# Output projection by seven products over four row pairs, and seven products of a weight pair gathered in one PSUM bank

## The chip, the cores and the metric

The kernel runs on one core of one Trainium2 chip. The metric is device time in microseconds (us) of one execution; smaller is better. Durations inside the execution come from one execution recorded by the hardware profiler.

## The reference, cut to what matters

A decoder block for one sequence of 1024 positions and D = 1024 channels, all in float32:

```python
h = rms_norm(x, norm_g)
proj = h @ w_in                      # u, g_rnn, q, k, v, g_attn, m_rnn, m_attn
u = causal_depthwise_conv(u, conv_w, conv_b)
y_rnn  = rg_lru(u, ...) * silu(g_rnn)
y_attn = sliding_window_attention_with_sinks(q, k, v, sinks) * silu(g_attn)
merged = sigmoid(m_rnn) * (y_rnn @ w_rnn_out) + sigmoid(m_attn) * (y_attn @ w_attn_out)
x = x + merged @ w_o
return rms_norm(x, final_norm_g)
```

## The kernel before, in words

**Precision.** Every float32 operand of a matrix product is split into a high part `h` (rounded to float32r by a ScalarE copy, L427) and a low part `l` (VectorE, `src - h`, L428). One 128x128 by 128x512 block product is then three matmuls: h·h, h·l, l·h.

**Pairs.** The weights of the input projection and of the two branch projections are cut into pairs. A pair is a 2x2 arrangement of blocks A11, A12, A21, A22 (128 output channels by 512 inputs each), and the right side is a 2x2 arrangement B11 ... B22 (512 inputs by 512 positions, each 4 tiles). `Pair.run` (L522) computes the 2x2 result by seven block products instead of eight, after Winograd: left sums S1 to S4 (L477), right sums T1 to T4 (L1004), seven products (L500, 12 matmuls each), and additions of products. Before the change these additions are five VectorE adds (u2, u3, c22, c21, c12) and one ScalarE copy (L517, of the first product), and a pair uses five PSUM banks, a to e. There are 32 such pairs: 8 `ug`, 2 `mr`, k, v, 4 `q`, 4 `ga`, 4 `ma`, 4 `zr` and 4 `za`. The right sides of one matrix (7 names x 4 tiles x 2 parts = 56 buffers) are built once and used by all its pairs: one for h, one for y_rnn (`zr`), one for y_attn (`za`).

**Merge.** `z_tail` (L1028) multiplies each finished block of `zr` and `za` with a gate loaded from DRAM (L1032) and, for `za`, adds it onto the `zr` block (L1041). That gives 16 tiles `MG[k, hf]`: channel tile k, half hf of the positions.

**Output projection.** The last stage (L1141 to L1174) splits all of MG (`mh`, `ml`) and of w_o (`Wh`, `Wl`), then goes through eight row blocks r of 128 positions. For each half c of the output channels it makes 8 block products of three matmuls into one bank (L1166, `three` at L567), adds x onto them (L1168), and after both halves it computes the root mean square (squares at L555 or L557, sum L561, root L563, reciprocal L564), scales (L1171) and stores (L1173). That is 8 x 2 x 8 x 3 = 384 matmuls.

**Order.** Nothing is issued in program order. Every operation is handed to a planner (`Plan.run`, L145) which lists it with its cost, its inputs and a priority, and writes out a fixed order for each engine; `TUNE` holds priorities and buffer limits, and `orders` the sequence of pairs and attention units. For work on TensorE the planner adds 1000 ns of slack after any input from another engine (L313). Buffers are 100 tiles of 128x512 in SBUF and 8 PSUM banks. Weight blocks are loaded through POOL's queue, everything else through SP's.

Of the kernel before, what the change touches and what calls it, by code (L numbers as in the profile page):

```python
# [11 lines left out]
F32R = mybir.dt.float32r  # L12
# [5 lines left out]
S = 1024  # L18
D = 1024
P = 128  # L20
# [12 lines left out]
    'm': (29, 2, 3),  # L33
# [4 lines left out]
    'zg': 3,  # L38
    'raw': 4,
    'raws': 9,  # L40
    'S': 4,
    'wc': 10,
    'B': 12,
    'psw': 67,
    'psk': 0,
    'Y': 8,
    'ld': 9,
    'lds': 21,
    'kv': 8,
    'kvs': 4,  # L50
    'qt': 4,
    'qts': 1,
    'P': 17,
    'AO': 22,
    'AOs': 12,
    'xo': 24,
    'lru0': 136,
    'xos': 11,
    'prep': 256,
    'att': 73,  # L60
    'val': 13,
    'gate': 1500,
    'lru': -1570,
    'qk': -147,
    'comb': 346,
    'ztl': -331,
    'xof': 47,
    'gzr': 21,
    'gza': 21,
    'gwo': 11,  # L70
    'gxo': 3,
    'gt': -6,
    'seven': 'ra',
    'mgd': 0,
# [268 lines left out]
def hybrid_block_kernel(ctx: ExitStack, tc: tile.TileContext, x, wall, wo, bd, vec, gfin,  # L343
# [16 lines left out]
                "P": (16, 0, 0, TUNE["P"]), "AO": (32, 0, 0, TUNE["AOs"]), "Y": (64, 0, 0, TUNE["Y"]), "zy": (TUNE["zy"], 0, 0, 0), "zg": (TUNE["zg"], 0, 0, 0), "wo": (32, 0, 0, TUNE["Y"]), "ld": (TUNE["ld"], 0, 0, TUNE["lds"]),  # L360
# [3 lines left out]
    def buf(cls, shape=None, dt=F32, name=None):  # L364
        return Buf(sp, "s2", cls, shape or [P, HF], dt, name or cls)
# [68 lines left out]
    def tt(dst, a, b, op, prio=0, eng=None):  # L434
        (eng or EW)(lambda e: e.tensor_tensor(dst.t, a.t, b.t, op=op), HF, [a, b], [dst], prio)  # L435
# [25 lines left out]
    class Pair:  # L461
# [3 lines left out]
        def __init__(self, i, comb, prio=None, cls="raw", by="POOL"):  # L465
            self.i, self.comb, self.prio, self.cls, self.A = i, comb, TUNE["prep"] if prio is None else prio, cls, {}
            self.W = {}
            self.by = by

        def raw(self, name):  # L470
            if name not in self.A:
                t = self.A[name] = buf(self.cls, name=name)
                b = ("A11", "A21", "A22", "A12").index(name)
                DMA(lambda: t.t, lambda: wall[self.i, b], 1 << 18, [], [t], self.prio, by=self.by)
            return self.A[name]

        def left(self, name):  # L477
            raw, prio, A = self.raw, self.prio, self.A
            if name[0] != "S":
                return raw(name)  # L480
            if name == "S1":
                return A["S1"]
            src = A[name] = buf("S", name=name)
            if name == "S2":
                s1 = A["S1"] = buf("S", name="S1")
                tt(s1, raw("A21"), raw("A22"), ADD, prio)
                tt(src, s1, raw("A11"), SUB, prio)
# [26 lines left out]
        def p1(self):  # L514
            self.a, self.c1 = bank("pair"), slot("p1")
            self.product(0, self.a, "A11", "B11", True)
            ACT(lambda q: q.copy(self.c1.t, self.a.t), HF, [self.a], [self.c1])  # L517

        def p2(self):
            self.product(2, self.a, "A12", "B21", False)  # L520
# [192 lines left out]
    def lru(c, C):  # L713
        (u0, u1), g = C
# [6 lines left out]
        hs = [None, None]  # L721
        for h, u in ((0, u0), (1, u1)):
# [24 lines left out]
            r, i, t, tg = (slot(n) for n in ("r", "i", "t", "tg"))  # L747
# [14 lines left out]
            gg = g[h]  # L762
            ACT(lambda e, tg=tg, gg=gg: e.activation(tg.t, gg.t, AF.Silu), HF, [gg], [tg], tset=SILU)
# [377 lines left out]
    WO = whole_from(lambda k, h: [((lambda: wo[k * P : (k + 1) * P, HALF[h]]), [])], [ahead(len(ids), TUNE["gwo"])], TUNE["comb"], "wo")  # L1141
    for h in range(2):
        for k in range(KT):
            WO(k, h)
    AO = {}
    for hf in range(2):
        for k in range(KT):
            AO[k, hf] = buf("AO", dt=F32R, name="mh")
            m = MG[k, hf]
            MG[k, hf] = buf("AO", dt=F32R, name="ml")  # L1150
            split_buf(AO[k, hf], MG[k, hf], m)
    gf_b = [load("xo", "gf_b") for _ in range(2)]
    for q in range(2):
        DMA(lambda q=q: gf_b[q].t, lambda q=q: gfin[HALF[q]].partition_broadcast(P), 1 << 18, [ahead(len(ids), TUNE["gxo"])], [gf_b[q]])
    for r in range(NB):
        xh = [load("xo", "xo") for _ in range(2)]
        for c in range(2):
            DMA(lambda c=c, xh=xh, r=r: xh[c].t, lambda c=c, r=r: x[r * P : (r + 1) * P, HALF[c]], 1 << 18,
                [ahead(len(ids), TUNE["gxo"])], [xh[c]], TUNE["xof"])
        w = slice(r % 4 * P, r % 4 * P + P)  # L1160
        for c in range(2):
            ps = bank("o")
            for k in range(KT):
                h, l = AO[k, r // 4], MG[k, r // 4]
                bh, bl = WO(k, c)
                PE(lambda ps=ps, h=h, l=l, w=w, bh=bh, bl=bl, k=k: three(ps, h, l, w, bh, bl, k == 0, k == KT - 1), 3,  # L1166
                   [h, l, bh, bl], [ps])
            tt(xh[c], ps, xh[c], ADD, 0, DVE)  # L1168
        rs = rstd_of(xh)
        for c in range(2):  # L1170
            DVE(lambda v, c=c, xh=xh, rs=rs: v.scalar_tensor_tensor(xh[c].t, xh[c].t, rs.t, gf_b[c].t, op0=MUL, op1=MUL), HF,  # L1171
                [xh[c], rs, gf_b[c]], [xh[c]], ptr=1)
            DMA(lambda c=c, xh=xh, r=r: out[r * P : (r + 1) * P, HALF[c]], lambda c=c, xh=xh: xh[c].t, 1 << 18, [xh[c]],  # L1173
                [("out", (r, c))])  # L1174
# [62 lines left out]
```

## Time and profile before

| | |
|---|---|
| Time, median of 3 runs | 901.39 us (901.3 to 901.75) |
| Time of the profiled execution | 901.53 us |
| Its span, first to last instruction | 899.8 us |
| PE busy | 874.7 us (97%) |
| VectorE (DVE) busy | 774.4 us (86%) |
| ScalarE (ACT) busy | 599.9 us (67%) |
| Mean granted TensorE clock | 0.99 |

The span is 1.7 us shorter than the time of the same execution; sums below are made in the span and then shifted. PE counts as busy while any matmul is in flight, and a matmul lasts longer than the distance to the next, so the rate is read from start to start.

### The profile page before, as it was taken

The page shows a single profiled execution, that of the slowest core. Times are in us where ns is not written, and L with a number is a line of the kernel's source. Part 1 is how long each engine was busy: PE and PEld are TensorE (multiplying, and loading weights), DVE is VectorE, ACT ScalarE, POOL GpSimd, SP SyncE. Part 2 cuts the span into 40 slices and gives each one's busy share as a digit, 9 for nine tenths or more (in the row PEclk, how much of TensorE's full clock was granted, in tenths as well). Part 3 has the DMA queues.
Part 4 walks back from the last instruction along what each step waited for, and adds up shares of the span by engine and source line. Part 5 has one row for each costly group of instructions (what it writes and reads, how often), then busy time and mean ns, then how long its engine had stood idle before and what let it go on. Part 6 is the DMA issues. An engine that isn't in the chain of part 4 may idle for free.

```text
span 899.8 us, 13035 instructions
## 1 busy us (share of the span) xinstructions
PE 874.7 (97%) x4088; PEld 721.8 (80%) x4088; DVE 774.4 (86%) x1579; ACT 599.9 (67%) x1232; POOL 72.9 (8%) x131
## 2 busy tenths in 40 slices
PE   4999999999999999999999999999999989999996
PEld 3778888878887888888888888888888868888885
DVE  6996999999996998888888888789999999897643
ACT  7655996996847777896498999999751444334000
POOL 2101010101000010011000000001100200000000
PEclk9999999999999999999999999999999979999999
DMA  9202146345641665256666445553857621682311
GB/s 327 104 34 83 58 119 173 111 140 145 164 129 48 194 193 139 72 138 213 171 173 188 132 130 176 146 158 89 268 184 244 207 74 50 208 297 78 117 47 47
DMA packets 86884, 129.75 MB, mean 144 GB/s; under 512 B 10656, under 2 KB 40224, under 8 KB 86816
## 3 DMA queue, kind: packets, MB, share of 16 engines
q1 hardware_dynamic: 77216, 97.47, 35.0%
q0 software_dynamic: 9600, 31.46, 12.1%
q8 instruction: 32, 0.52, 0.2%
q14 instruction: 36, 0.29, 0.1%
HBM read 87.21 MB, written 41.68 MB: 143 GB/s over the span
## 4 chain that ended last, share of the span: by engine, by line
PE 63%; DVE 3%; ACT 3%; issue 1%; DVEq 0%
PE pair L508 15%; PE pair L509 15%; PE pair L510 15%; PE o L569 3%; PE o L570 3%; PE o L568 3%; PE ps_s L899 3%; PE ptp L933 3%; PE po L947 1%; PE po L946 1%; ACT sm L914 1%; ACT sm L922 1%; DVE wl L428 1%; DVE cu L728 0%; ACT ph L427 0%
## 5 line engine op out<-in xcount | busy, mean ns | idle before, releaser
L418 POOL DMA_DIRECT2D A<-in_wall_dram x120 | 64.5, 538 | 676.6 <-PE pair L510 169.4
L427 ACT CAST wh<-S 128x512 fp32r<-128x512 f32 x128 | 78.3, 616 | 41.2 <-DVE S L435 27.6
L428 DVE TENSOR_TENSOR wl<-S,wh 128x512 fp32r<-128x512 f32 x128 | 87.6, 686 | 7.9 <-ACT wh L427 6.7
L435 DVE TENSOR_TENSOR c<-pair,u 128x512 f32<-128x512 f32 x96 | 65.6, 686 | 7.0 <-PE pair L510 6.4
L428 DVE TENSOR_TENSOR wl<-A,wh 128x512 fp32r<-128x512 f32 x96 | 65.9, 687 | 1.7 <-ACT wh L427 1.1
L427 ACT CAST wh<-A 128x512 fp32r<-128x512 f32 x96 | 59.3, 617 | 12.1 <-PE pair L510 6.3
L914 ACT ACTIVATE sm<-sm,nm 128x256 f32<-128x256 f32 (+1 forms) x128 | 61.9, 487 | 1.8 <-DVE nm L907 1.6
L922 ACT ACTIVATE sm<-sm,dn 128x256 f32<-128x256 f32 (+1 forms) x128 | 53.9, 489 | 1.8 <-DVE dn L919 0.9
L907 DVE CUSTOM_DVE_ANT_0 sm<-ps_s,mask_t,sink_t 128x256 f32<-128x256 f32 (+1 forms) x128 | 53.8, 459 | 1.0 <-PE ps_s L899 1.0
L509 PE MATMUL pair<-B21l,wh 128*128 128x512 f32 x128 | 51.2, 400 | 1.1 <-DVE B21l L428 1.1
L508 PE MATMUL pair<-B11h,wh 128*128 128x512 f32 x128 | 51.7, 404 | 0.5 <-DVE B12l L424 0.5
L508 PE MATMUL pair<-B21h,wh 128*128 128x512 f32 x128 | 51.9, 406 | 0.3 <-ACT B21h L427 0.3
L509 PE MATMUL pair<-T2l,wh 128*128 128x512 f32 x128 | 50.0, 391 | 1.9 <-DVE T2l L428 1.9
L563 ACT ACTIVATE sd<-ss,eps_t 128x1 f32<-128x1 f32 x16 | 4.3, 289 | 71.1 <-DVE ss L561 71.1
L508 PE MATMUL pair<-B22h,wh 128*128 128x512 f32 x128 | 51.0, 398 | 0.8 <-DVE c L435 0.8
L510 PE MATMUL pair<-B21h,wl 128*128 128x512 f32 x128 | 50.9, 398 | 0.0
L508 PE MATMUL pair<-T3h,wh 128*128 128x512 f32 x128 | 50.7, 396 | 0.0
L508 PE MATMUL pair<-T4h,wh 128*128 128x512 f32 x128 | 50.7, 396 | 0.0
L508 PE MATMUL pair<-T1h,wh 128*128 128x512 f32 x128 | 50.6, 396 | 0.0
L509 PE MATMUL pair<-B11l,wh 128*128 128x512 f32 x128 | 50.5, 394 | 0.0
L510 PE MATMUL pair<-B11h,wl 128*128 128x512 f32 x128 | 50.3, 393 | 0.0
L508 PE MATMUL pair<-T2h,wh 128*128 128x512 f32 x128 | 50.1, 392 | 0.0
(222 smaller groups left out, 2606.2 us busy)
## 6 DMA issues: line engine op xcount, KB each, us to landing
A<-in_wall_dram POOLq DMA_DIRECT2D x120, 256.0 KB, 3.2
qt<-st_q SPq DMA_DIRECT2D x32, 256.0 KB, 3.5
xt<-in_x_dram SPq DMA_DIRECT2D x16, 256.0 KB, 5.4
A<-in_wall_dram SPq DMA_DIRECT2D x16, 256.0 KB, 5.4
tm_r<-tm SPq DMA_DIRECT2D x16, 256.0 KB, 2.2
yr_dr<-tg SPq DMA_DIRECT2D x16, 256.0 KB, 2.2
K<-st_k SPq DMA_DIRECT2D x32, 128.0 KB, 3.6
st_q<-qh SPq DMA_DIRECT2D x32, 128.0 KB, 2.9
```

Of the source, the lines that this page charges most:

```text
L418: pl.op([("POOL", 1000.0)], reads, writes, lambda e: nc.gpsimd.dma_start(dst(), src()), prio, move=move)
L427: ACT(lambda e: e.copy(h(), src()), cols, reads, wh, prio)
L428: (DVE if psum else EW)(lambda e: e.tensor_tensor(l(), src(), h().bitcast(F32), op=ALU.subtract), cols, list(reads) + list(wh), wl, prio)
L435: (eng or EW)(lambda e: e.tensor_tensor(dst.t, a.t, b.t, op=op), HF, [a, b], [dst], prio)
L508: nc.tensor.matmul(ps.t, h.t[:, w], bh.t, start=start and k == 0, stop=False, **kw)
L509: nc.tensor.matmul(ps.t, h.t[:, w], bl.t, start=False, stop=False, **kw)
L510: nc.tensor.matmul(ps.t, l.t[:, w], bh.t, start=False, stop=k == 3, **kw)
L568: nc.tensor.matmul(ps.t, h.t[:, w], bh.t, start=start, stop=False)
L569: nc.tensor.matmul(ps.t, h.t[:, w], bl.t, start=False, stop=False)
L907: DVE(lambda v, ps=ps, j=j, h=h, s=s: v.tensor_tensor_reduce(s.t[:, j, :], ps.t[:, j, :], att["mask"].t[:, 256 - w : 256], scale=-0.125, s ...
L914: ACT(lambda e, h=h, s=s, j=j: e.activation(s.t[:, j, :], s.t[:, j, :], AF.Exp, scale=-1.0, bias=nm.t[:, h : h + 1], accum_out=dn.t[:, h : ...
L922: ACT(lambda e, h=h, s=s, j=j: e.activation(s.t[:, j, :], s.t[:, j, :], AF.Identity, scale=dn.t[:, h : h + 1]), w, [(s, j), dn], [(s, j)], ...
```

## The change

Three things happen. (1) `Pair.run` gathers five of the seven products of a pair in one bank `a`, with ScalarE copies of the running sum in between (c1, u2, u3); A12·B21 goes into a second bank b and the two products that share B-sides T1 and B22 into a third, d. The order of products becomes 0, 4, 1, 2, 3, 5, 6. (2) The output projection is computed with the same seven products, each over four row blocks (four banks) at once, so that its left sides are the four 4-tile blocks of MG, and its right side is w_o through `comb_from`. (3) Nearly all of `TUNE` takes new values, with a new sequence of pairs and units; in `lru` both Silu activations move ahead of the convolution, and for the eight `ug` pairs the two rows of the pair change places (`turned`). `pre` is 0, so `first` is false throughout.

```diff
-    'raw': 4,
+    'raw': 5,
...
-    'S': 4,
-    'wc': 10,
-    'B': 12,
-    'psw': 67,
+    'S': 5,
+    'wc': 11,
+    'B': 11,
+    'psw': 92,
...
-    'gzr': 21,
-    'gza': 21,
-    'gwo': 11,
+    'gzr': 14,
+    'gza': 44,
+    'gwo': 14,
...
         def run(self):
-            self.p1()
-            a, c1 = self.a, self.c1
-            b, c, d, e = (bank("pair") for _ in range(4))
+            a, b, d = (bank("pair") for _ in range(3))
             u2, u3 = slot("u2"), slot("u3")
-            c12, c21, c22 = slot("c12"), slot("c21"), slot("c22")
-            self.product(1, b, "S2", "T2", True)
-            tt(u2, b, c1, ADD, 0, DVE)
-            self.p2()
-            self.product(3, c, "S3", "T3", True)
-            tt(u3, c, u2, ADD, 0, DVE)
+            c12, c22 = slot("c12"), slot("c22")
+            first = TUNE["pre"]
+            self.product(0, a, "A11", "B11", True)
+            c1 = b if first else slot("c1")
+            ACT(lambda q: q.copy(c1.t, a.t), HF, [a], [c1])
             self.product(4, d, "S1", "T1", True)
+            self.product(1, a, "S2", "T2", False)
+            ACT(lambda q: q.copy(u2.t, a.t), HF, [a], [u2])
+            self.product(2, b, "A12", "B21", not first)
+            c11 = b
+            if not first:
+                c11 = slot("c11")
+                tt(c11, b, c1, ADD, 0, DVE)
+            self.product(3, a, "S3", "T3", False)
+            ACT(lambda q: q.copy(u3.t, a.t), HF, [a], [u3])
             tt(c22, d, u3, ADD, 0, DVE)
-            self.product(5, e, "A22", "T4", True)
-            tt(c21, e, u3, ADD, 0, DVE)
+            self.product(5, a, "A22", "T4", False)
             self.product(6, d, "S4", "B22", False)
             tt(c12, d, u2, ADD, 0, DVE)
-            return [[a, c12], [c21, c22]]
+            return [[c11, c12], [a, c22]]
...
+    WO = comb_from(lambda k, h: [((lambda: wo[k * P : (k + 1) * P, HALF[h]]), [])], [ahead(len(ids), TUNE["gwo"])], TUNE["comb"])
+    blk = {n: [MG[k + 4 * q, h] for k in range(4)] for n, q, h in (("A11", 0, 0), ("A21", 0, 1), ("A12", 1, 0), ("A22", 1, 1))}
+    def total(n, a, b, op):
+        blk[n] = [buf("AO", name=n) for _ in range(4)]
+        for k in range(4):
+            tt(blk[n][k], blk[a][k], blk[b][k], op, TUNE["lo"])
+    def product_o(ps, a, b, start):
+        L = [(buf("AO", dt=F32R, name="mh"), buf("AO", dt=F32R, name="ml")) for _ in range(4)]
+        for k in range(4):
+            split_buf(*L[k], blk[a][k], TUNE["lo"])
+        R = WO(b)
+        for i in range(4):
+            for k in range(4):
...
+                    nc.tensor.matmul(ps.t, h.t[:, w], bh.t, start=start and k == 0, stop=False, **kw)
+                    nc.tensor.matmul(ps.t, h.t[:, w], bl.t, start=False, stop=False, **kw)
+                    nc.tensor.matmul(ps.t, l.t[:, w], bh.t, start=False, stop=k == 3, **kw)
...
+    a, d = four(), four()
+    product_o(a, "A11", "B11", True)
+    c1 = kept("c1", a)
+    total("S1", "A21", "A22", ADD)
+    product_o(d, "S1", "T1", True)
+    total("S2", "S1", "A11", SUB)
+    product_o(a, "S2", "T2", False)
+    u2 = kept("u2", a)
+    total("S3", "A11", "A21", SUB)
+    product_o(a, "S3", "T3", False)
+    u3 = kept("u3", a)
+    for i in range(4):
+        XO[i + 4, 1] = x_rows(i + 4, 1)
+        tt(u3[i], d[i], u3[i], ADD, 0, DVE)
+        tt(XO[i + 4, 1], XO[i + 4, 1], u3[i], ADD)
+    total("S4", "A12", "S2", SUB)
+    product_o(d, "S4", "B22", False)
+    for i in range(4):
+        XO[i, 1] = x_rows(i, 1)
+        tt(u2[i], d[i], u2[i], ADD, 0, DVE)
+        tt(XO[i, 1], XO[i, 1], u2[i], ADD)
...
+    product_o(a, "A22", "T4", False)
+    for i in range(4):
+        XO[i + 4, 0] = x_rows(i + 4, 0)
+        tt(XO[i + 4, 0], a[i], XO[i + 4, 0], ADD, 0, DVE)
+        row_out(i + 4, [XO[i + 4, 0], XO[i + 4, 1]])
+    for i in range(4):
+        XO[i, 0] = x_rows(i, 0)
+        tt(c1[i], XO[i, 0], c1[i], ADD)
+    b = four()
+    product_o(b, "A12", "B21", True)
+    for i in range(4):
+        tt(XO[i, 0], b[i], c1[i], ADD, 0, DVE)
+        row_out(i, [XO[i, 0], XO[i, 1]])
```

`kept` copies four banks to SBUF on ScalarE, and `row_out` is the tail of a row block as before: squares, root, reciprocal, two scalings, two stores.

## Rows read from the trace of the kernel before

**Rows 1.** The page, part 1: busy us, share, instructions of each engine.

```profile
PE 874.7 (97%) x4088; PEld 721.8 (80%) x4088; DVE 774.4 (86%) x1579; ACT 599.9 (67%) x1232; POOL 72.9 (8%) x131
```

**Rows 2.** Stretches of the span: busy time, granted clock, DMA share, GB/s.

```profile
0.00:47.00 47.00, 33.67 (x160) 27.46 (x160) 37.66 (x107) 34.28 (x73) 8.39 (x11) 0.96 0.58 208
47.00:300.00 253.00, 251.63 (x1099) 204.77 (x1100) 227.29 (x371) 188.56 (x286) 22.66 (x42) 1.00 0.38 108
300.00:645.00 345.00, 344.89 (x1777) 289.70 (x1776) 299.47 (x739) 296.40 (x728) 30.05 (x56) 1.00 0.56 162
645.00:721.10 76.10, 76.10 (x336) 62.60 (x335) 74.90 (x125) 33.16 (x60) 7.47 (x14) 1.00 0.68 218
721.10:805.60 84.50, 81.19 (x337) 65.34 (x336) 81.46 (x134) 33.72 (x61) 4.29 (x8) 0.94 0.42 142
805.60:893.00 87.40, 87.20 (x385) 71.91 (x383) 50.66 (x104) 13.46 (x27) 0.00 (x0) 1.00 0.24 87
```

**Rows 3.** Timeline of one product: start us, duration us, engine, instruction.

```profile
770.02 0.39 PE L510 MATMUL pair<-B11h,wl 128*128 128x512 f32 x1
...
770.24 0.39 PE L508 MATMUL pair<-T2h,wh 128*128 128x512 f32 x1
...
770.44 0.59 ACT L517 COPY p<-pair 128x512 f32<-128x512 f32 x1 [4.52 <-PE pair L510]
...
772.96 0.39 PE L508 MATMUL pair<-B21h,wh 128*128 128x512 f32 x1
```

**Rows 4.** Stretches inside 721.1 to 805.6 us, columns as in Rows 2.

```profile
724.00:728.50 4.50, 2.61 (x12) 1.82 (x11) 4.50 (x8) 1.11 (x2) 0.00 (x0) 1.00 0.00 0
728.50:739.00 10.50, 9.08 (x21) 5.94 (x20) 10.50 (x19) 5.83 (x11) 1.08 (x2) 0.51 0.16 51
739.00:749.00 10.00, 10.00 (x46) 8.28 (x45) 10.00 (x18) 6.51 (x13) 1.07 (x2) 1.00 0.08 27
```

**Rows 5.** Timeline of DVE and PE at the first `za` pair.

```profile
726.73 1.29 DVE L428 TENSOR_TENSOR T2l<-T,T2h 128x512 fp32r<-128x512 f32 x2
...
727.47 0.50 PE L509 MATMUL pair<-T2l,wh 128*128 128x512 f32 x1 [1.89 <-DVE T2l L428]
...
732.88 0.80 PE L509 MATMUL pair<-B21l,wh 128*128 128x512 f32 x1 [0.76 <-DVE B21l L428]
...
736.35 1.90 DVE L435 TENSOR_TENSOR T<-YB,YB 128x512 f32<-128x512 f32 x3
738.15 1.90 DVE L428 TENSOR_TENSOR T3l<-T,T3h 128x512 fp32r<-128x512 f32 x3
```

**Rows 6.** Copy L517: itself; idle before it; who waited for it (us, times).

```profile
L517 ACT COPY p<-pair x32: 563/586/607, 72.6 to 789.5; 128x512 f32<-128x512 f32 x32
...
  PE pair L510: 15.8, 10
...
  PEld pair L508: 0.5, 2
```

**Rows 7.** One of the DVE groups of the whole span: busy us, mean ns | idle before.

```profile
L435 DVE TENSOR_TENSOR u<-pair,p 128x512 f32<-128x512 f32 x32 | 22.0, 688 | 3.0 <-PE pair L510 2.1 <-PE ptp L933 0.6 <-ACT p L517 0.2
```

**Rows 8.** PE groups of 805.6 to 899.8 us; the other two lines are alike.

```profile
L570 PE MATMUL o<-Wh,ml 128*128 128x512 f32 x128 | 49.8, 389 | 0.0
```

**Rows 9.** DVE groups of 805.6 to 899.8 us.

```profile
L435 DVE TENSOR_TENSOR xo<-o,xo 128x512 f32<-128x512 f32 x16 | 11.1, 691 | 33.5 <-PE o L570 33.5
```

**Rows 10.** Timeline of the last 8 us.

```profile
892.42 0.39 PE L570 MATMUL o<-Wh,ml 128*128 128x512 f32 x1
892.84 0.69 DVE L435 TENSOR_TENSOR xo<-o,xo 128x512 f32<-128x512 f32 x1 [4.01 <-PE o L570]
...
895.02 1.42 DVE L1171 SCALAR_TENSOR_TENSOR xo<-xo,rs,gf_b 128x512 f32<-128x512 f32 x2
```

**Rows 11.** Timeline of PE where two `za` pairs meet.

```profile
783.84 0.39 PE L508 MATMUL pair<-B11h,wh 128*128 128x512 f32 x1
...
785.88 0.39 PE L508 MATMUL pair<-B22h,wh 128*128 128x512 f32 x1
```

More of the change, by code (lines that the diff above doesn't have):

```diff
@@ L32 @@
 TUNE = {
-    'm': (29, 2, 3),
+    'm': (29, 3, 3),
     'slack': (1000.0, 1500.0),
@@ L37 @@
     'zy': 7,
-    'zg': 3,
-    'raw': 4,
+    'zg': 2,
+    'raw': 5,
     'raws': 9,
-    'S': 4,
-    'wc': 10,
-    'B': 12,
-    'psw': 67,
+    'S': 5,
+    'wc': 11,
+    'B': 11,
+    'psw': 92,
     'psk': 0,
-    'Y': 8,
+    'Y': 10,
     'ld': 9,
-    'lds': 21,
+    'lds': 25,
     'kv': 8,
     'kvs': 4,
-    'qt': 4,
-    'qts': 1,
+    'qt': 3,
+    'qts': 3,
     'P': 17,
     'AO': 22,
-    'AOs': 12,
+    'AOs': 18,
     'xo': 24,
[L57 to L67, printed above, removed]
-    'gzr': 21,
-    'gza': 21,
-    'gwo': 11,
+    'lru0': -183,
+    'xos': 10,
+    'prep': 244,
+    'att': 91,
+    'val': 95,
+    'gate': 893,
+    'lru': -1188,
+    'qk': -306,
+    'comb': 349,
+    'ztl': 300,
+    'xof': 497,
+    'gzr': 14,
+    'gza': 44,
+    'gwo': 14,
     'gxo': 3,
-    'gt': -6,
+    'gt': -5,
     'seven': 'ra',
+    'pre': 0,
+    'sil': 100,
+    'lo': 0,
     'mgd': 0,
[3 rows of a table removed]
[3 rows of a table added]
 }
@@ L468, in __init__ @@
             self.by = by
+            self.turned = i < U_MR
         def raw(self, name):
@@ L472, in raw @@
                 t = self.A[name] = buf(self.cls, name=name)
-                b = ("A11", "A21", "A22", "A12").index(name)
+                b = (("A21", "A11", "A12", "A22") if self.turned else ("A11", "A21", "A22", "A12")).index(name)
                 DMA(lambda: t.t, lambda: wall[self.i, b], 1 << 18, [], [t], self.prio, by=self.by)
@@ L480, in left @@
                 return raw(name)
+            src = A[name] = buf("S", name=name)
             if name == "S1":
[L482 to L487, printed above, removed]
+                tt(src, raw("A21"), raw("A22"), ADD, prio)
+            elif name == "S2":
+                tt(src, A["S1"], raw("A11"), SUB, prio)
             elif name == "S3":
@@ L721, in lru @@
         hs = [None, None]
+        tgs = []
+        for gg in g:
+            tgs.append(slot("tg"))
+            ACT(lambda e, tg=tgs[-1], gg=gg: e.activation(tg.t, gg.t, AF.Silu), HF, [gg], [tgs[-1]], TUNE["sil"], tset=SILU)
         for h, u in ((0, u0), (1, u1)):
@@ L1138, in hybrid_block_kernel @@
         pl.bias = 0
[L1141 to L1151, printed above, removed]
+    at_end = [ahead(len(ids), TUNE["gxo"])]
@@ new lines, in kept, with x_rows, row_out @@
+    def kept(name, src):
+        out_ = [slot(name) for _ in range(4)]
+        for i in range(4):
+            ACT(lambda e, d=out_[i], s=src[i]: e.copy(d.t, s.t), HF, [src[i]], [out_[i]])
+        return out_
+    def x_rows(r, c):
+        t = load("xo", "xo")
+        DMA(lambda: t.t, lambda: x[r * P : (r + 1) * P, HALF[c]], 1 << 18, at_end, [t], TUNE["xof"])
+        return t
+    def row_out(r, xh):
+        rs = rstd_of(xh)
+        for c in range(2):
+            DVE(lambda v, c=c: v.scalar_tensor_tensor(xh[c].t, xh[c].t, rs.t, gf_b[c].t, op0=MUL, op1=MUL), HF,
+                [xh[c], rs, gf_b[c]], [xh[c]], ptr=1)
+            DMA(lambda c=c: out[r * P : (r + 1) * P, HALF[c]], lambda c=c: xh[c].t, 1 << 18, [xh[c]], [("out", (r, c))])
@@ new lines, in hybrid_block_kernel @@
+    four = lambda: [bank("o") for _ in range(4)]
+    XO = {}
+    a, d = four(), four()
[13 more added lines that the diff above has]
+        tt(XO[i + 4, 1], XO[i + 4, 1], u3[i], ADD)
@@ new lines, in hybrid_block_kernel @@
+        DMA(lambda q=q: gf_b[q].t, lambda q=q: gfin[HALF[q]].partition_broadcast(P), 1 << 18, at_end, [gf_b[q]])
+    product_o(a, "A22", "T4", False)
[8 more added lines that the diff above has]
+    product_o(b, "A12", "B21", True)
+    for i in range(4):
+        tt(XO[i, 0], b[i], c1[i], ADD, 0, DVE)
+        row_out(i, [XO[i, 0], XO[i, 1]])
```

39 lines of the change are left out of this document (7 added, 32 removed), and 6 rows, old and new, of the table TUNE.

## The prediction

> **What bounds the kernel now.** I read the page's first part, then the span cut into stages, then PE's start times, then the places where PE lost time. The page says PE 97%, DVE 86%, ACT 67% [rows 1]. A busy PE proves little, so the second step is its rate. One product of twelve matmuls runs from 770.24 to 772.96 us, 2.72 us, or 0.227 us for each matmul of 512 columns [rows 3]. The `zr` stage, 4 pairs x 7 products x 12 = 336 matmuls, takes 76.1 us for 336 matmuls, which is exactly that rate (336 x 0.227 = 76.2) [rows 2]. So do the 384 matmuls of the output projection (87.2 us in 87.4, no idle before any of them) [rows 2, 8]. From 47 us to 721 us PE is idle for under 2 us in all [rows 2]. TensorE's issue rate is the bound almost everywhere; what is left over is four places:
> - the start, 47 us with only 160 instructions of PE;
> - the first `za` pair. The `za` stage has the same 336 matmuls as `zr` but takes 84.5 us, 8.3 us more [rows 2]. PE waits 1.89 us for `T2l` and later 0.76 us for `B21l`, both splits on DVE [rows 5], and then runs 10.5 us at a granted clock of 0.51, that is 1.2 GHz, with 21 matmuls where the next 10 us hold 46 [rows 4]. The gap came first, the slow clock after it. DVE was the late engine: 74.90 of 76.10 us busy in `zr`, and 4.5 of 4.5 and 10.5 of 10.5 us at the gap [rows 2, 4];
> - small gaps between 47 and 300 us (251.63 of 253.00 busy) [rows 2];
> - the tail: the last matmul starts at 892.42 us [rows 10], the span ends at 899.8.
>
> **The change part by part.**
>
> *Matmuls.* Seven products over four banks are 7 x 4 x 4 x 3 = 336 matmuls in place of 384. 48 x 0.227 = **10.9 us** leave the engine that bounds, from a stage that runs at its rate. The pairs keep their 7 x 12 matmuls. Bounds: at most 10.9; less only by new waits, priced below.
>
> *DVE and ACT in a pair.* Five DVE adds become three; u2 and u3 are now copies on ACT [rows 7]. Back to back a DVE operation of 512 columns takes 0.60 us (three from 736.35 to 738.15) [rows 5], so DVE gets 1.2 us back per pair and 32 x 1.2 = 38 us over the kernel. Where PE is the bound that is worth nothing. Where DVE was late it counts: `zr` has four pairs, 4.8 us less DVE work ahead of the `za` splits, and loading of y_attn may start earlier (`gza` 44 products ahead, 21 before). At full rate B21l would have been wanted about 5 us before it came, so 4.8 us nearly closes the gap, and with the gap goes the slow clock. Bounds: 0 to 8.3 us gained. I take **5.3**, about two thirds, since T1 must now be ready a product earlier than B21 and the new order is not known in the trace.
>
> *ACT.* Two more copies of 0.59 us a pair. In 300 to 645 us, the attention stage, ACT is busy 296 of 345 us [rows 2]; thirteen or fourteen pairs lie there, so about 16 us are added to 49 us of room. The planner fixes ACT's order, and a copy placed ahead of its product makes the casts behind it wait, and behind these the DVE low parts and PE's weights: the one copy of before held ACT idle for 15.8 us in ten places and PE for 0.5 us in two [rows 6]. Three copies scale that to 1.5 us of PE. I take **1.0 us lost**.
>
> *The new waits inside a pair.* Product S2·T2 waits for copy c1, with S1·T1 (2.72 us) between; S3·T3 waits for u2, with A12·B21 between. But after S3·T3 the two products left both wait for u3: A22·T4 adds onto the bank being copied, and S4·B22 onto d, whose sum c22 needs u3. Nothing of the pair itself covers this one. Its price when bare: the matmul at 770.02 would be followed at 770.25; the copy instead starts at 770.44 and lasts 0.59 [rows 3], and PE follows a release within about 0.05 us (T2l done by 727.4, PE at 727.47) [rows 5], so the next starts at 771.08, 0.83 us late. The cover is the next pair's first product: three banks a pair instead of five leave two or three of eight for it, and the planner's 1000 ns of slack on PE's inputs exceeds 0.83. So nothing beyond the 1.0 us above; the bound is 32 x 0.83 = 27 us, a rival below. In the output stage each product goes through four banks, so a copy has 8 us of cover.
> The Trainium skill, page "PSUM — Partial Sum Buffer", section "Summary: rules for kernel authors", speaks against the change here: for reading PSUM while a matmul runs it says to target a different bank. The rows agree that a product into a copied bank must wait, but show 0.5 us in 32 copies where another product stands between. By the rule with nothing between, the time is that of the second rival.
>
> *The output stage's DVE work.* Before, it makes 32 low parts, 16 adds, 16 squares and 16 scalings, and DVE is busy 50.7 of 87.4 us, 33.5 us idle waiting for PE [rows 2, 9]. After: 28 left and 28 right low parts, 16 left sums, 16 right sums, 28 adds of results, 16 scalings: 132 x 0.60 = 79 us, and some 3 us of small ones, against 76.2 us of PE. It fits only if part is done ahead. In `za` DVE's own work falls to 4 x 22 operations = 53 us of 76, but of the 100 SBUF tiles the `za` right side holds 56, MG 16, and weights about 20, so perhaps 16 to 20 operations (10 to 12 us) can be ahead. That leaves 70 of 76 us. Per product: the middle ones need 4+4 left and 4+4 right operations = 9.6 us, inside the 10.9 us a product takes. S1 needs the very last `za` block: add, gate, add, sum, cast, low part, six steps of 0.6, some 4 us, under the 10.9 us of A11·B11. So no wait is forced, yet there is little room: I take **2.0 us lost**, bounds 0 to 16 (rival).
>
> *Tail.* The last row block still ends with add, square, root, scaling and store, 7 us after PE [rows 10]. But the last four row blocks now finish 2.72 us apart, not 10.9, and one takes 3.6 us from its add to its last scaling (892.84 to 896.44) [rows 10]. Unless the planner overlaps them, 3 x 0.9 = 2.6 us pile up; DVE's share of a block is about 2.4 us, so mostly they do. **0.5 us lost**. The eight stores of the last four blocks, 2 MB in 10.9 us, are 190 GB/s; `zr` moved 218 [rows 2].
>
> *Hidden or without cost.* The 16 loads of w_o and 16 of x are the same in number on SP's queue. Silu earlier and the swapped rows of `ug` move work within the stretch where PE lacks under 1.4 us. The start is governed by x's arrival and the first splits, which the diff leaves alone; T1 is now wanted second, but S2·T2 and A12·B21 can go first.
>
> **Sum.** 899.8 - 10.9 - 5.3 + 1.0 + 2.0 + 0.5 = 887.1 us of span, plus 1.7 outside it = 888.8; the profiled execution lies 0.14 us above the median: **888.7 us**.
>
> **Rivals.**
> 1. *All stalls go.* The `za` gap closes whole and nothing new opens: 899.8 - 10.9 - 8.3 + 1.6 = 882.2. For it: DVE's 38 us. Against: the output stage's tightness. Chance 0.17.
> 2. *Bare u3 copies (slower).* If the planner has no other pair to fill with after S3·T3, each of 32 pairs loses 0.83 us: 888.7 - 1.0 + 26.6 = 914 us. It decides from (12.7 + 1.0) / 0.83 = 17 of 32 pairs on. For it: `wc` holds five factors, so the next pair's must be in early; against: a new pair's B11 product already stands before the old pair's B22 product [rows 11], and 0.5 us of waits in 32 [rows 6]. Chance 0.08.
> 3. *DVE sets the pace of the output stage.* Nothing is ready at its start: 8 splits first, 4.8 us; the gap drops the clock, which costs 4.3 us (25 matmuls short [rows 4], less the 1.4 us of waits in that stretch); then the last three products need 20, 20 and 26 operations, 12.0, 12.0 and 15.6 us against 10.9, 7 us more. 888.7 - 2.0 + 16.1 = 902.8: no change, and slower if `za` keeps its gap too. Chance 0.12.
> 4. The new order of attention and pairs starves PE somewhere between 47 and 645 us, where hardly anything is lost today: some 5 to 15 us, 894 to 904. Chance 0.08.
>
> **How the numbers follow.** The forecast, 883 to 894, has 0.55. The range 880 to 898 takes in rival 1 and part of 3 and 4; about 0.05 lies below and 0.15 above. A measurement of this kernel tells 0.2%, 1.8 us, from no change. Faster: 0.55 + 0.17 and most of 3 and 4 = 0.84; same 0.06; slower 0.10 (rival 2 and the ends of 3 and 4).
>
> **What the profile of the changed kernel would show.** 336 matmuls of `o` in about 76 to 79 us; DVE 90% or more busy there. The `za` stage at 77 to 80 us, with a shorter stretch at half clock or none. DVE's total nearly unchanged (38 us off the pairs, about 40 more in the output stage), ACT some 60 us higher. PE's waits for ACT's u3 copies under 2 us. I am wrong if PE shows a wait after S3·T3 in many pairs, if a second stretch at half clock appears near the start of the output stage, or if the tail is over 10 us.

## The result, and the profile after

The changed kernel takes 896.51 us (median of 4 runs, 896.38 to 896.95) against 901.57 for the kernel before on the same chip: a ratio of 0.9946, 95% interval 0.9931 to 0.9961. That is faster by 0.5%, and the whole interval lies below 1. It is inside the range of 880 to 898, but 5.1 us were gained where 12.7 were forecast. The span is 894.5 us, the granted clock 0.993.

The page's first part of the changed kernel, in answer to [rows 1]:

```profile
PE 862.4 (96%) x4040; PEld 711.5 (80%) x4040; DVE 772.0 (86%) x1571; ACT 633.0 (71%) x1326; POOL 73.0 (8%) x131
```

There are 48 matmuls less, and VectorE's total is almost the same, as expected. In what follows, products, sums and banks have the names of the code above (A11·B11, S1, `mh`, `ml`, c22). The stretches of the changed kernel, with the columns of [rows 2]; `za` is 726.7 to 805.3, the output projection 805.3 to 886.1, the last line the tail:

```profile
0.00:47.00 47.00, 33.81 (x160) 27.25 (x160) 37.97 (x106) 34.07 (x73) 9.03 (x12) 0.96 0.61 216
47.00:300.00 253.00, 250.76 (x1107) 205.59 (x1108) 218.89 (x357) 186.32 (x304) 22.87 (x43) 1.00 0.36 105
300.00:640.00 340.00, 337.19 (x1725) 282.26 (x1724) 269.75 (x682) 290.80 (x716) 28.17 (x53) 1.00 0.57 162
640.00:726.70 86.70, 86.70 (x389) 71.53 (x388) 83.69 (x145) 47.49 (x93) 9.14 (x17) 1.00 0.62 203
726.70:805.30 78.60, 75.37 (x329) 60.98 (x329) 77.48 (x127) 37.66 (x69) 3.76 (x7) 1.00 0.48 165
805.30:886.10 80.80, 78.55 (x337) 63.85 (x335) 79.57 (x148) 36.03 (x73) 0.00 (x0) 0.98 0.20 72
886.10:894.50 8.40, 0.00 (x0) 0.00 (x0) 4.70 (x12) 0.59 (x2) 0.00 (x0) 0.66 0.51 187
```

Read PE stage by stage against [rows 2]:

| | before | after | difference | forecast |
|---|---|---|---|---|
| matmuls, 48 x 0.227 | | | -10.9 | -10.9 |
| PE idle from 0 to 640 us (645 before) | 14.8 | 18.2 | +3.4 | +1.0 |
| `za`, lost against 0.227 a matmul | 8.2 | 4.3 | -3.9 | -5.3 |
| output stage, lost against 0.227 a matmul | -0.1 | 4.4 | +4.5 | +2.0 |
| last matmul's start to the end | 7.4 | 8.8 | +1.4 | +0.5 |
| sum | | | -5.5 | -12.7 |

The row of PE's idle time is the busy column subtracted from the stretches; the two below it sum the distances from each matmul's start to the next, less the usual one. The span fell by 5.3 us; the rows are rounded and read in different ways, which leaves 0.2. All four terms beside the matmuls came out worse than forecast, the output stage by the most. The row of `za` has two things in it: the gap at the first pair, and a wait for a copy in the last; they are told apart below.

What PE waited for from 640 us to the end (us in all, times, longest):

```profile
PE o L1164 <- DVE ml L431: 2.2, 2, 2.1
PE pair L511 <- DVE T2l L431: 1.6, 1, 1.6
PE pair L512 <- DVE wl L431: 1.0, 1, 1.0
PE pair L510 <- ACT u L533: 0.7, 1, 0.7
```

The first line is the output stage's first product, A11·B11. DVE's timeline ahead of it, of the changed kernel:

```profile
807.34 0.69 DVE L1034 SCALAR_TENSOR_TENSOR tz<-tz,pair 128x512 f32<-128x512 f32 x1
808.06 0.69 DVE L438 TENSOR_TENSOR tz<-tz 128x512 f32<-128x512 f32 x1
...
814.57 0.69 DVE L1034 SCALAR_TENSOR_TENSOR tz<-tz,c 128x512 f32<-128x512 f32 x1
...
815.90 0.68 DVE L431 TENSOR_TENSOR ml<-tz,mh 128x512 fp32r<-128x512 f32 x1
```

and PE's:

```profile
814.18 0.39 PE L1163 MATMUL o<-B11l,mh 128*128 128x512 f32 x1
816.64 0.50 PE L1164 MATMUL o<-B11h,ml 128*128 128x512 f32 x1 [2.07 <-DVE ml L431]
...
817.24 0.63 PE L1163 MATMUL o<-B11l,mh 128*128 128x512 f32 x1
817.67 0.63 PE L1164 MATMUL o<-B11h,ml 128*128 128x512 f32 x1
```

The last six `za` blocks, twelve DVE operations from 807.34 on (a product with the gate and an addition each), stand in DVE's order ahead of the fourth `ml` of A11, which PE wants at 814.4. Their gates were issued last on SP's queue (six loads, 802.05 to 805.7), behind fourteen loads of x and the two of `gf_b`; the chain that ended last goes through one of them ("802.05 5.26 DMA tz<-tm_a"). DVE itself idled for the gates for only 0.2 us. PE waits 2.1 us, and then starts a matmul every 0.43 us instead of 0.227: the slower of the clock's two levels, 1.2 GHz. Over the stretch, and from there to PE's end:

```profile
814.40:820.60 6.20, 4.13 (x11) 3.12 (x11) 6.17 (x11) 3.10 (x6) 0.00 (x0) 0.72 0.28 91
820.60:886.10 65.50, 65.49 (x289) 53.87 (x287) 64.58 (x124) 31.80 (x65) 0.00 (x0) 1.00 0.14 49
```

Behind that place PE is at its rate again (289 matmuls in 65.5 us) and waits for nothing up to its end, though DVE is full there, with 64.58 of 65.50 us busy. That is the answer to [rows 9], where it had 33.5 us of room. Some of its groups from 805.3 us to the end:

```profile
L431 DVE TENSOR_TENSOR ml<-S,mh 128x512 fp32r<-128x512 f32 x16 | 10.4, 683 | 0.0
L431 DVE TENSOR_TENSOR ml<-tz,mh 128x512 fp32r<-128x512 f32 x12 | 7.8, 682 | 0.0
L556 DVE CUSTOM_DVE_ANT_0 junk<-xo 128x512 f32<-128x512 f32 x10 | 6.9, 692 | 0.2
...
L438 DVE TENSOR_TENSOR tz<-tz 128x512 f32<-128x512 f32 x6 | 4.2, 692 | 0.2
L1034 DVE SCALAR_TENSOR_TENSOR tz<-tz,c 128x512 f32<-128x512 f32 x4 | 2.7, 683 | 0.0
```

The end of DVE's work, in answer to [rows 10] (PE's last matmul starts at 885.71):

```profile
886.41 0.68 DVE L438 TENSOR_TENSOR xo<-o,c 128x512 f32<-128x512 f32 x1
...
887.12 0.69 DVE L556 CUSTOM_DVE_ANT_0 junk<-xo 128x512 f32<-128x512 f32 x1
...
887.74 1.41 DVE L1182 SCALAR_TENSOR_TENSOR xo<-xo,rs,gf_b 128x512 f32<-128x512 f32 x2
...
889.78 1.42 DVE L1182 SCALAR_TENSOR_TENSOR xo<-xo,rs,gf_b 128x512 f32<-128x512 f32 x2
```

Upstream, the two longest waits of PE from 300 to 640 us are new; before, PE was idle for 0.11 us in that stage [rows 2]:

```profile
PE pair L510 <- ACT u L526: 1.3, 1, 1.3
PE pair L510 <- DVE c L438: 0.7, 1, 0.7
```

ACT around the first of them:

```profile
411.48 0.62 ACT L430 CAST wh<-S 128x512 fp32r<-128x512 f32 x1 [4.97 <-PE pair L512]
412.12 0.59 ACT L526 COPY u<-pair 128x512 f32<-128x512 f32 x1
```

A weight cast that waits for PE to free its buffer stands ahead of the copy u2 that PE waits for: ACT is idle for 4.97 us while the copy behind the cast can't be issued.

### The profile page after: what moved, and what is told of

Same layout as the page of the kernel before. It is cut to its first block, busy times and chain, and to the rows that moved or that the text cites. A ratio compares the mean times of both kernels' runs of the same rounds, so it can differ in the third digit from the quotient of the medians.

```text
span 894.5 us, 13047 instructions
## 1 busy us (share of the span) xinstructions
PE 862.4 (96%) x4040; PEld 711.5 (80%) x4040; DVE 772.0 (86%) x1571; ACT 633.0 (71%) x1326; POOL 73.0 (8%) x131
## 4 chain that ended last, share of the span: by engine, by line
PE 62%; DVE 24%; ACT 8%; issue 4%; DMA 2%; SPq 0%; DVEq 0%; ACTq 0%
PE pair L510 17%; PE pair L511 16%; PE pair L512 16%; PE ps_s L901 3%; DVE cu L731 2%; PE ptp L935 2%; DVE hs L764 2%; DVE wl L431 2%; ACT sm L916 2%; DVE ml L431 2%; DVE S L438 2%; DVE c L438 1%; ACT sm L924 1%; PE fd L568 1%; PE fd L567 1%
## 5 line engine op out<-in xcount | busy, mean ns | idle before, releaser
L431 DVE TENSOR_TENSOR wl<-A,wh 128x512 fp32r<-128x512 f32 x96 | 65.5, 683 | 4.7 <-ACT wh L430 3.1
L438 DVE TENSOR_TENSOR c<-pair,u 128x512 f32<-128x512 f32 x64 | 43.8, 684 | 8.8 <-ACT u L533 4.6
L512 PE MATMUL pair<-T4h,wl 128*128 128x512 f32 x128 | 50.0, 390 | 0.0
L511 PE MATMUL pair<-T3l,wh 128*128 128x512 f32 x128 | 50.0, 390 | 0.0
L512 PE MATMUL pair<-T2h,wl 128*128 128x512 f32 x128 | 50.0, 390 | 0.0
L511 PE MATMUL pair<-B22l,wh 128*128 128x512 f32 x128 | 49.9, 390 | 0.0
```

The costliest lines, as they stand in the source:

```text
L431: (DVE if psum else EW)(lambda e: e.tensor_tensor(l(), src(), h().bitcast(F32), op=ALU.subtract), cols, list(reads) + list(wh), wl, prio)
L511: nc.tensor.matmul(ps.t, h.t[:, w], bl.t, start=False, stop=False, **kw)
L512: nc.tensor.matmul(ps.t, l.t[:, w], bh.t, start=False, stop=k == 3, **kw)
```

## The experiments

Two theories to begin with. **D**: VectorE's amount of work, from the join of `za` and the output stage on, sets the end; a late piece that is moved comes up at another place. **P**: single late pieces, ahead of the first product above all, cost PE the time; put right, they give it back. Kernels with names in `f_` keep the order of the changed kernel, written out once, and edit it: `after(op, ref)` puts one operation directly behind another. In kernels with names in `p_` the planner draws a new order. Ratios are to the kernel before on the same chip. Where an excerpt of code gives a condition in words, the run tests operation numbers; "..." marks what is left out.

**f_ml**: the late low part moved directly behind its cast.

```diff
+        after(4434, 4433)   # fourth ml of A11 behind its mh
```

> The changed kernel with its written-out order kept, but the fourth low part of A11 in the output projection (a VectorE subtraction) is put right behind its cast, ahead of the VectorE work on the six late gate blocks. Theory D: VectorE is full from 805 us to the end, so the wait of PE for that low part is only where VectorE's lateness shows first; the 2.2 us wait goes from the A11*B11 product and comes back as a wait of 2 to 4 us ahead of the S1*T1 product, and the time stays at 896.5, within 1 us. Rival P: PE is the bound and the 4.4 us lost at that wait (2.2 us of it at half clock) are the loss itself; they go, and the time falls to 892 to 893 us.

896.06 us, 0.9942 (0.9927 to 0.9957): no gain that can be told, as D expected. PE's wait for the fourth low part went, and came back at the next product, S1·T1, with the slow clock behind it (0.72 from 820 to 826 us). The first line is the first low part of A11, for which the changed kernel waits 0.17 us:

```profile
806.73 0.50 PE L1172 MATMUL o<-B11h,ml 128*128 128x512 f32 x1 [1.19 <-DVE ml L439]
...
818.40 0.50 PE L1170 MATMUL o<-T1h,mh 128*128 128x512 f32 x1 [0.96 <-ACT mh L438]
...
820.10 0.73 PE L1172 MATMUL o<-T1h,ml 128*128 128x512 f32 x1 [0.97 <-DVE ml L439]
```

**f_sq**: the ten squares that the planner had given to DVE go to ACT.

```diff
+        order = [(i, 'ACT' if i is a square of row_out else e) for i, e in order]
```

> The changed kernel in its written-out order, but the ten sums of squares of the output rows that VectorE makes are made on ScalarE, 0.77 us each off VectorE after 850 us. Theory D: the wait at the first product stays (it lies before any square), PE has no wait after it, so PE ends at the same time and only the tail behind PE gets shorter, from 8.6 us to about 7.2: 895 us. Rival V: VectorE's sum alone sets the end, so the 7.7 us taken off it move the end by 5 us or more, to 891 or less. Rival P: no change, 896.5.

895.46 us, 0.9930 (0.9916 to 0.9945). Some 7 us of DVE's work are gone from the second half and 1.0 us from the median, with intervals that overlap those of the changed kernel. That is near what D expected (895), and far from rival V (891 or less): DVE's work in the second half doesn't set the end one for one. In the profiled execution, the fastest of four (893.85 us), the tail fell from 8.8 to 8.0 us, the wait at the first product stayed (2.2 us), and the clock did not fall behind it.

**f_more**: eight DVE operations more in the output stage.

```diff
+            if i in (4605, 4608, 4611, 4614, 4653, 4656, 4659, 4662):   # the additions of x
+                b = next(b for b in o["bufs"] if b.name == "xo")
+                tc.nc.vector.tensor_tensor(self.spare, b.t, b.t, op=ALU.add)
```

> The changed kernel in its written-out order with eight more VectorE operations of 128x512 in the output projection (x + x into a tile that nobody reads), one behind each addition of x to a result between 845 and 865 us. Theory D (VectorE has no idle time from 805 us to the end): 8 x 0.6 us = 4.8 us go onto the end, 901 us, with PE ending at the same time or with new waits. Rival P (PE is the bound, VectorE's fullness is only the planner using free time): under 1 us, 897.

901.46 us, 1.0015 (1.0002 to 1.0028). PE's last matmul starts at 883.01, no later than in the changed kernel (the clock did not fall in this execution), and the end lies 15.3 us behind it, where it was 8.8. 8 x 0.69 = 5.5 us of added work are some 6 us of time by the ratios (0.0069 x 901), all of it behind PE: an operation added to DVE here costs about its whole length. With f_sq this says that the two engines end the stage close together: more work on DVE shows in full, less of it gains only until PE's rate is the floor.

**f_join, f_joinsq**: three of the six late gate loads and their gate products brought forward, f_ml's move, and the low parts of T2, sums of T3 and the first additions of x put back; the second with the squares on ACT.

```diff
+        for op, ref in ((4353, 4350), (4356, 4353), (4415, 4356),      # gate loads
+                        (4354, 4352), (4355, 4354), (4357, 4355), ...  # gate products
+                        (4532, 4478), (4534, 4532), ...                # T2's low parts
+                        (4750, 4575), (4752, 4750)):                   # x + c1
+            after(op, ref)
```

> The changed kernel's order with one region reordered: three of the six late gate loads are issued ahead of the loads of x, their gate products on VectorE are made as soon as the data are there, the fourth low part of A11 comes right behind its cast, and eight VectorE operations that later products need (the low parts of T2, three sums of T3, two additions of x) go behind the split of S1. The same instructions, only their order differs. Theory D: the wait at A11*B11 and the half clock go and PE ends about 4 us earlier, but VectorE has as much to do as before and the tail behind PE grows by most of that: 893.5 to 896. Rival P: the order was the whole loss: 892 us. Rival V: no change.

> Both edits together: the reordered start of the output projection, and the ten sums of squares on ScalarE. Theory D: now PE neither waits at the start nor has VectorE behind it at the end, so the two gains meet: PE ends about 4.4 us earlier and the tail is about 7.2 us, 890.5 to 891.5 us, more than the sum of the two alone. Rival P: the same as the reordering alone, 892. Rival V: as the squares alone.

901.82 (1.0005, 0.9993 to 1.0017) and 901.34 us (1.0000, 0.9987 to 1.0013): both missed by far. PE's waits in f_join:

```profile
PE o L1178 <- DVE ml L445: 3.9, 1, 3.9
PE pair L524 <- DVE c L452: 2.9, 1, 2.9
```

The wait at the first product is gone; PE now waits for the sum c22 of the last `za` pair and for a low part of S2. The lateness was moved, and grew. But part of it is made by the new order: DVE, which in the changed kernel is never idle for long there, waits 3.4 us in all for ScalarE's casts in f_join, most of it here:

```profile
817.55 0.69 DVE L445 TENSOR_TENSOR ml<-S,mh 128x512 fp32r<-128x512 f32 x1 [2.02 <-ACT mh L444]
```

So these two don't show that no order of the same work would do better; they show one that does worse.

**f_pool**: the squares on ACT, f_ml's move, and sixteen additions on GpSimd.

```diff
+        away = {4571, 4572, 4573, 4574, 4750, ...}   # T3, T4, S3, x + c1
+        order = [(i, 'POOL' if i in away else e) for i, e in order]
```

> The changed kernel in its written-out order with 26 operations off VectorE in the output projection: the ten sums of squares on ScalarE, and sixteen SBUF additions with time to spare (sums of T3 and T4, differences S3, additions of x to c1) on GpSimd, which is idle there; the fourth low part of A11 also right behind its cast. Theory D: some 17 us of VectorE work leave the stage, five of these operations ahead of the first two products, so the waits there shrink by about 3 us and the tail by 1.2 us: 890.5 to 892.5 us. Rival: GpSimd takes 1.2 us or more for one and holds VectorE up while both read SBUF, and a later sum comes late in its turn: 895 or slower. Rival P: 892 (only the waits).

901.97 us, 1.0017 (1.0007 to 1.0027): missed. Groups of POOL, and two of DVE from 800 to 830 us (busy, mean ns):

```profile
L449 POOL TENSOR_TENSOR S<-tz 128x512 f32<-128x512 f32 x4 | 9.6, 2421 | 6.4 <-PE o L1174 6.4
...
L449 POOL TENSOR_TENSOR T<-YB,YB 128x512 f32<-128x512 f32 x4 | 6.4, 1618 | 23.6 <-DVE tz L449 23.6
```

```profile
L442 DVE TENSOR_TENSOR ml<-S,mh 128x512 fp32r<-128x512 f32 x4 | 5.8, 1498 | 0.0
...
L442 DVE TENSOR_TENSOR T1l<-T,T1h 128x512 fp32r<-128x512 f32 x2 | 3.1, 1612 | 0.0
```

The same low parts take 0.68 us in the changed kernel. What left DVE for GpSimd came back in part as longer operations on DVE, and the sums on GpSimd take over twice as long as on DVE (spans on GpSimd are rough in a profile). The rival named beforehand was right.

**f_cut, f_cut2**: to take DVE's work away rather than move it, parts of the computation are left out, with the squares on ACT.

```diff
-                o["fn"](e)
+                if i not in (4355, 4358, 4417, 4420, 4423, 4426):   # f_cut; f_cut2: 8 more
+                    o["fn"](e)
```

> Based on the version with the squares on ScalarE (895.5 us). Leaves out the last six additions of za blocks onto zr blocks, so that these tiles of MG hold the zr part alone: 6 x 0.72 = 4.3 us less on VectorE between 807 and 816 us. Theory D (VectorE's work sets the output stage): PE's wait at the second product goes, PE needs 76 to 77 us for its 336 matmuls, the tail shrinks towards 7.4 us: 891.2 us. Rival P (the stage's loss comes from the order or from ScalarE): 894.5 us or more.

> As the cut of six additions, and leaves out the eight additions of x to the results of the right half too: 8 x 0.69 = 5.5 us less on VectorE in the second half of the output stage. Theory D: with VectorE no longer the later engine PE's rate is the floor: 805.3 + 76.2 + 7.4 + 2.0 = 890.9 us, next to nothing below the cut of six alone. If VectorE's work counted one for one to the end: 885.7 us. Rival P: 894.5 us or more.

890.86 us, 0.9886 (0.9870 to 0.9903), and 892.12 us, 0.9901 (0.9882 to 0.9921). The first is what D expected. Output stage and tail of f_cut, in the columns of [rows 2]:

```profile
805.30:881.10 75.80, 75.67 (x334) 62.61 (x334) 70.05 (x124) 41.61 (x89) 0.00 (x0) 1.00 0.21 73
881.10:889.10 8.00, 0.37 (x2) 0.00 (x0) 3.82 (x8) 1.31 (x4) 0.00 (x0) 0.68 0.53 197
```

PE runs near its rate from end to end (one wait of 0.6 us is left; A11·B11 loses 1.0 us by its start times, where it lost 4.4) and DVE has 5.8 us of room. The first cut, 4.3 us at the join, is worth 4.0 by the ratios of f_sq and f_cut (0.0044 x 901); a further 5.5 us, taken later in the stage, nothing. With DVE out of the way PE's rate is the floor. The work that was cut was also the late work, so f_cut by itself does not tell amount from place; f_ml does in part: there the low part that stood behind the late work came early, and nothing was gained.

**f_up**: with the squares on ACT, four upstream places reordered.

```diff
+        for op, ref in ((2444, 2165),                # cast behind the u2 copy, 412 us
+                        (878, 969), (981, 1072), (1084, 1175), (1085, 1084)):   # lru: ul first
+            after(op, ref)
```

> Based on the version with the squares on ScalarE (895.5 us). Four places between 229 and 412 us are reordered: in three lru steps the low part of u goes ahead of the product with the gate, and at 412 us the copy of u2 goes ahead of a cast of weights that waits for PE to free its buffer. PE's waits there are 0.6, 0.7, 0.3 and 1.3 us, 2.9 us in all. Theory U (what PE loses upstream passes whole to the end): 892.5 us. Rival A (the lost time is absorbed by VectorE's full stretch from 640 us on, which can't start earlier): 895.5 us.

894.1 us (891.63 to 895.28), 0.9920 (0.9900 to 0.9939): between the two (892.5 and 895.5), and neither is told from the other. The edits did less than they should. Of PE's 1.6 us for `ul` 1.2 are left, the 1.3 us at u2 became 0.7, and the sum c costs 0.6. Two of the lines of f_up, 47 to 640 us:

```profile
PE psb L755 <- DVE ul L441: 1.2, 2, 0.8
PE pair L520 <- ACT u L536: 0.7, 1, 0.7
```

It has the lowest median of the versions that leave nothing out; its interval overlaps that of f_sq, so it can't be called better than that one.

**f_za, f_zcut, f_zcut_cut**: the gap at the first `za` pair. The first moves gate products of `zr` behind the splits, the second leaves nine of them out, the third is both cuts; all have the squares on ACT.

```diff
+        for op, ref in ((4028, 4150), (4030, 4028), (4034, 4030), (4225, 4122)):   # f_za
+            after(op, ref)
```

> Based on the version with the squares on ScalarE (895.5 us). Three of the four products of zr blocks with their gates, which stand ahead of the four low parts of T2 at 728 us, go behind the low parts of B21, and a weight's low part directly behind T2's. T2l is 1.8 us earlier, so PE's waits of 1.6 us for T2l and 1.0 us for the weight and the half clock behind them should go. Theory L (one late place): the stretch 730 to 736.4 us, with 17 matmuls where 28 fit, gets its 2.5 us back: 893 us. Rival M (VectorE is late as a whole there; the wait moves to the next split): 895.5 us or more, with a new wait for B21l or S1 some 5 to 8 us later.

> Based on the version with the squares on ScalarE (895.5 us, PE 5.3 us short of its rate in the za stage). Leaves out the product with the gate for nine blocks of zr between 693 and 730 us, so that these hold the gate alone: 9 x 0.6 = 5.4 us less on VectorE ahead of the first za splits. Theory M (VectorE is late as a whole at the first za pair): the waits for T2l and for the weight and the half clock behind them go, za comes down to about 77.5 us, and what PE gains there passes to the end: 892.0 us. Rival S (the output stage's VectorE work keeps the end where it is, or a wait comes back at another split): 895 us.

> Both cuts: the nine gate products of zr and the six additions of za are left out, 9.7 us of VectorE's work in all. If the za gap and the output stage's loss are both VectorE's lateness: 890.9 - 3.5 = 887.4 us, about what was forecast for the change. Rival S (the gain at za is absorbed later): 890.5 us or more.

f_za: 894.74 us, 0.9932 (0.9917 to 0.9947), the ratio of f_sq, as rival M expected. The wait for T2l is gone; what PE waits for now in `za`:

```profile
PE pair L521 <- DVE B21l L441: 0.9, 1, 0.9
...
PE pair L522 <- DVE wl L441: 0.7, 1, 0.7
```

f_zcut: 894.09 us (892.07 to 896.02), 0.9925 (0.9905 to 0.9945), between M (892.0) and S (895), and not told from f_sq. In its profile PE doesn't wait for T2l and starts 24 matmuls from 730 to 736.4 us, against 17 in the changed kernel; but the 2 us wait at A11·B11 is there again, and half clock behind it. What the gap costs on its way to the end stays open. (The half clock that the expectations name at the `za` gap is not in the changed kernel: its granted clock is 1.00 there, and 17 matmuls in place of 28 are the two waits.) Together with the cut at the join, 890.09 us, 0.9884 (0.9863 to 0.9906): no less than f_cut by these intervals, and nearer to rival S (890.5 or more) than to 887.4.

**p_out, p_oldout, p_pair, p_tune**: one part of the change at a time, whole blocks exchanged between the two kernels. p_out is the kernel before with the new output projection and the old constants; p_oldout the changed kernel with the old output projection; p_pair the new pairs and the new `lru` order with the old constants and the old output projection; p_tune the kernel before with the new constants.

> The kernel before with the new output projection alone (its pairs, constants and order of pairs as before; the limit of AO tiles at 48). Planned anew. Theory D: PE gets 10.9 us less work, but VectorE keeps five additions a pair, so the wait at the first za pair stays (8 us) and the output stage, 80 us of VectorE work for 76 us of PE, loses 5 to 10 us at its start and end: 896 to 901 us. Rival P: the whole 10.9 us come, 890 to 891.

> The changed kernel with the old output projection (new pairs, new constants and order). Planned anew. Theory D: the output stage has free VectorE time again and runs its 384 matmuls without a wait; the 10.9 us come back, the 5.9 us lost at start and tail of the new stage go: 901 to 902 us, and the stages before za lose about 3 us against the kernel before, since they are the same as in the changed kernel. Rival: the new output projection gains nothing net of its waits, 896 to 898.

> The new pairs and the new lru order alone, with the output projection and the constants of before; the planner draws a new order. By the prediction's terms for the pairs, -5.3 + 1.0: 897 us. Rival (constants and pairs hang together: an order drawn with the old constants gives PE waits for copies and splits): 901.5 us or more, with waits of over 5 us in all between 300 and 806 us.

> The kernel before with the new constants alone: no part of the computation is changed. If the constants are what cost PE time upstream (3 us more lost ahead of za than before): 904 us. If the copies of the pairs are what costs it, the constants alone leave the upstream part as it was: 901.5 us.

911.31 us (1.0114, 1.0099 to 1.0129), 909.37 (1.0096, 1.0078 to 1.0113), 927.92 (1.0301, 1.0286 to 1.0316) and 950.8 (1.0556, 1.0540 to 1.0571). Every part alone makes the kernel slower. PE's longest waits of the first two after 640 us:

```profile
PE o L1163 <- ACT T2h L430: 12.2, 1, 12.2
```

```profile
PE pair L512 <- DVE wl L431: 7.7, 2, 6.8
```

No wait of this length is in the changed kernel behind its first 50 us: they come from the order that the planner drew for a mix that its constants were not made for. p_tune changes nothing that is computed and costs 50 us, where its two theories said 904 and 901.5. So these four say what an order is worth, and can't be read as the price of a part; the expectations that were sums of terms (p_out, p_oldout, p_pair) took no account of that. For the same reason they don't settle whether the copies or the order cost the time upstream.

## Why the prediction was wrong in size

- **Matmuls, -10.9**: right. 48 less, and the rate did not change (289 in 65.5 us).
- **Output stage, 2.0 lost: the step that failed.** 4.4 were lost. "That leaves 70 of 76 us" and "So no wait is forced" are mis-sized: from 805.3 us to the end DVE has 79.57 + 4.70 = 84.3 us of work. Two things were left out of the sum. It counts no squares, though the sentence before it lists sixteen on DVE, and the planner gave ten to DVE (6.9 + 0.8 us). And thirteen operations of `za` run inside the stage (about 8.6 us): the six late blocks, whose gates are loaded last, and the last c22. Both could be read in the kernel before, from 805.6 us on:

```profile
L557 DVE CUSTOM_DVE_ANT_0 junk<-xo 128x512 f32<-128x512 f32 x16 | 11.1, 692 | 0.5
...
L435 DVE TENSOR_TENSOR tz<-tz 128x512 f32<-128x512 f32 x4 | 2.8, 692 | 0.1
```

The credit for work done ahead was about right (12 right low parts and 10 right sums, 22 operations, against 16 to 20). With DVE full there was no room, so a late piece cost PE a wait and a slow clock at the first product; one of the three signs of being wrong that the prediction named, half clock near the start of the output stage, came. f_ml shows that the piece put early only shifts the wait, f_cut that with 4.3 us less at the join PE runs near its rate, f_more that work added later comes out at the end. That a better order of the same work would not help is argued, not shown. The third rival had the first half of this, splits late at the start and the clock behind them, at 9.1 us for 4.4; its second half, 7 us in the last three products, did not come: PE lost nothing there.

- **Tail, 0.5 lost**: 1.4. A square of the last row block and the two scalings of the one before it (887.12, 887.74) stand on DVE ahead of the last block's root; with the squares on ACT it is 0.6 (8.0 against 7.4).
- **`za` gap, 5.3 gained**: 3.9 for the stage, but 5.2 at the gap itself. By the start times the first pair lost 8.3 us before (723.83 to 740.32) and loses 3.2 now (730.15 to 738.75). The slow clock went as said (1.00 in `za` now, 0.94 before [rows 2]), and with it most of the gap. The wait for `T2l` stayed, at 1.6 us for 1.89 [rows 5], since DVE is 83.69 of 86.70 us busy ahead of it. f_za says that it is late as a whole there: a split moved forward makes the next one late. That 5.2 is so near 5.3 is in part luck: the third that was held back was meant for T1, and what is left stands at T2l and at a weight. What the stage lost beside that is mainly the bare copy u3 of the last pair, below.
- **Upstream, 1.0 lost**: 3.4. The 0.5 us of [rows 6] were read as PE's; they are PEld's, the weight load's, and PE shows no wait for that copy. The mechanism named is seen once at length: a copy behind a blocked cast, 1.3 us at 412 us; with 0.2 for a copy c1 it makes 1.5 us, near the 1.0. The rest is DVE's and stood in no term: the sum c22 at 303 us (0.7), three lru steps (1.6), where `ul` stands behind the product with the gate, and small waits. The new `lru` order had been put at nothing ("Hidden or without cost"). That the copies and the `lru` order cost it, and not the planner's order under the new constants, was not shown: f_up took away too little, p_pair and p_tune lost far more at other places. This cause stays open.
- **u3 copies**: right in price, and nearly in number. Only one of 32 pairs, the last, has nothing between, and it pays what was worked out, 0.84 us (0.83), which the sum had at nothing:

```profile
798.65 0.39 PE L512 MATMUL pair<-T3h,wl 128*128 128x512 f32 x1
...
799.08 0.59 ACT L533 COPY u<-pair 128x512 f32<-128x512 f32 x1 [2.41 <-PE pair L512]
...
799.72 0.50 PE L510 MATMUL pair<-T4h,wh 128*128 128x512 f32 x1 [0.68 <-ACT u L533]
```

The rule weighed there (the Trainium skill, page "PSUM — Partial Sum Buffer", section "Summary: rules for kernel authors": target a different bank while one is read) agrees with the trace in this one pair, where PE waits to add onto the bank being copied. In the others another product or work of the attention units stands between.

- **ACT some 60 us higher**: 33 us. The 64 further copies of the pairs alone are 64 x 0.58 = 37, and the output stage adds casts and copies. Against that, ACT loads its function tables 46 times where it did 64 times, at 1.28 us each: 18 x 1.28 = 23 us less. With both Silu of an `lru` step together, eight loads of each kind there do what fourteen did. The prediction had the Silu down as work that only moves.

## What to carry to other kernels

Where a change trades the bound engine's work for another's, sum up the second engine's work in that stage with all that can spill in: late pieces of the stage before, and operations that a planner may place on either engine. When the sum nears the stage's length, moving a late operation forward made the next one late here, and what helped was less work on that engine at the place where it was late. Don't price one part of a change by building it alone where an order is redrawn from constants: the new order may cost more than the part.

## What was not expected of the hardware

- An addition of 128x512 on GpSimd took 1.62 to 2.42 us, and low parts on DVE in the same stretch 1.50 to 1.61 us instead of 0.68.
- After a wait of about 2.1 us at the same place the clock fell in the changed kernel (0.72 from 814.4 to 820.6 us) and not in f_sq (2.2 us, 1.00 over the same stretch). After waits of 1.9 us there it fell in f_up and f_zcut (0.72) and not in f_more and f_za (1.00). What decides it stays open; the time of a single execution has some 2 us of such luck in it.
- A product with the gate and the addition that reads it start 0.72 us apart (807.34, 808.06), where operations that don't depend on each other start every 0.60 us.
